# Two ties and eight row products moved in VectorE's order, in a two-layer decoder trunk

## The chip, the cores and the metric

The kernel runs on one core of one Trainium2 chip. The metric is the device time of one execution in microseconds (us). Before the change it is 683.57 us, the median of 3 runs (683.51 to 684.01).

The core has five engines that run side by side, each through its own list of instructions in a fixed order: TensorE (PE in the profile; PEld is its loading of weights), VectorE (DVE), ScalarE (ACT), GpSimd (POOL) and SyncE (SP), which here only issues loads. They wait for each other on semaphores.

## The reference, cut to what matters

Two layers work on 256 tokens of width 1024, all in float32. Each layer has a mixer and an MLP. Both begin with an RMSNorm whose result is scaled and shifted by numbers worked out from a conditioning vector c:

```python
mod = c_act @ w_ada[l] + b_ada[l]
sh_m, sc_m, gt_m, sh_f, sc_f, gt_f = jnp.split(mod[:, None, :], N_MOD, axis=-1)
h = rms_norm(x, g_pre_mix[l]) * (1.0 + sc_m) + sh_m
y = token_mixer(h, w_in[l], g_moba_out[l], g_dsa_out[l], w_out[l], cos, sin)
x = x + gt_m * rms_norm(y, g_post_mix[l])
h = rms_norm(x, g_pre_ffn[l]) * (1.0 + sc_f) + sh_f
y = conv_glu_ffn(h, w_up_act[l], w_up_lin[l], w_conv[l], b_conv[l], w_down[l])
x = x + gt_f * rms_norm(y, g_post_ffn[l])
```

The mixer projects h onto 3656 columns and runs two groups of attention heads: MoBA (at 256 tokens plain causal attention) and DSA, in which an indexer gives each query a score for each key and only the 64 best keys are attended. The MLP is down(gelu(conv3(h @ w_up_act)) * (h @ w_up_lin)).

## The kernel before, in words

**Split products.** Every large product runs in three passes of a reduced float32 type: each operand is split into a high part and a low rest, and hi*hi + hi*lo + lo*hi is summed in PSUM. `split` (L124 to L143) makes the parts of 128x1024 weights: ScalarE writes the high part (L141), VectorE the low one (L142). Low and high tiles are named wh/wl (5 of each) or dh/dl. A weight tile `raw` holds 128x2048 numbers; six of them rotate, and SyncE issues the next load (L114) when one comes free.

**Modulation.** c times w_ada is a vector times a matrix. Part of it is done on VectorE: `gemv_v` (L183 to L194) loads a tile of transposed weights and multiplies 1024 columns by the row of c, with a running sum, one *row product* (L190) for each 128 outputs. In the first layer columns 24 to 31 of `mods` are the MLP's shift (eight products), 32 to 39 the MLP's scale (eight more), 40 to 47 the MLP's gate.

**Order of the work.** The program is written out by hand. A `Background` object holds chains of generators; at every step of the main work it ticks, and a chain that has counted down issues its next piece. A planner (the Tile scheduler) then lays each engine's list: it takes, among what it holds to be ready, what was written first. So an instruction that is ready early floats forward past earlier work that waits. There are three ways to hold it: `tc.issue_after(ins)` puts what is written in its block behind `ins` on the same engine; `pin` keeps program order; and `queue` (L352 to L358) ties each instruction to the one queued before it. None of them adds a wait: they set the order of the list. The queue holds VectorE's rotations (`rope_out`, L366, L371) and the rounds of the choice (`choose`, L450 to L460: eight rounds of MAX8 at L454 and MATCH_REPLACE at L455 for each of two token tiles).

**First layer's mixer.** While TensorE projects mv, dq, dk, dv (`project`, L388 to L413), the background runs the transposes, the indexer (L424 to L448), the choice and the attention (`attend`, L462 to L552): score products into banks 4 and 5 (L474), VectorE's mask and row minimum (L484), ScalarE's exponentials (L488), VectorE's normalising (L491, L496), transposes (L503), value products (L519). The score products of the next set need both banks back from L484.

**From mixer to MLP.** `out_first` and `out_last` are the output projection; `out_last` ends with token tile 1. `boundary` (L333 to L350) follows: for each token tile the residual (L319, L327), the statistic (L255, then GpSimd's L263 and L265), the norm on VectorE (L287), transposes (L275), modulation (L298, L301, L306 to L310). Then `project(l, "lin", ...)` takes the first four column blocks of w_up_lin as one 512-column projection: eight k of 128 rows, in four units of two k. For token tile 0 it runs hi*hi and hi*lo of k = 0 to 7 in turn, then lo*hi of all eight (`late="h"`). Matmuls into one bank stay in the order written. The four units are split ahead of `out_last` (L911), the fourth (k = 6 and 7) into wh/wl.

Of the kernel before, what the change touches and what calls it, by code (L numbers as in the profile page):

```python
# [10 lines left out]
F32 = mybir.dt.float32  # L11
# [63 lines left out]
def trunk(ctx: ExitStack, tc, plan, x, c, stream, small, rope, out):  # L75
    nc = tc.nc
# [28 lines left out]

    st = {"off": 0, "behind": ()}

# [16 lines left out]
    def split(raw, where=None, pin=False, gain=None):  # L124
# [7 lines left out]
        with ExitStack() as behind:  # L132
# [8 lines left out]
            put(nc.scalar.activation(out=hi[:, :n], in_=raw, func=AF.Copy))  # L141
            put(nc.vector.tensor_tensor(out=lo[:, :n], in0=raw, in1=hi[:, :n].bitcast(F32), op=OP.subtract))  # L142
        return hi, lo  # L143
# [38 lines left out]

    def gemv_v(l, j0, j1, gap, behind=None):  # L183

        for j in range(j0, j1, 2):
            r = load(("v_a", l, j, 2048))[0]
            for i in range(2):
                ri = r[:, 1024 * i:1024 * i + 1024]
                with tc.issue_after(behind) if behind else ExitStack():
                    nc.vector.scalar_tensor_tensor(out=ri, in0=ri, scalar=1.0, in1=crow, op0=OP.mult, op1=OP.mult,  # L190
                                                   accum_out=mods[l][:, j + i:j + i + 1])
                yield gap
        nc.vector.tensor_tensor(out=mods[l][:, j0:j1], in0=mods[l][:, j0:j1],
                                in1=scol(l, "b_ada")[:, j0:j1], op=OP.add)  # L194
# [89 lines left out]
    def norm_T(t, r, banks):  # L284
        xn = [t2(), t2()]
        for h in range(2):
            nc.vector.tensor_scalar(out=xn[h], in0=xt[:, t, 512 * h:512 * h + 512], scalar1=r, scalar2=None,  # L287
                                    op0=OP.mult)
        return [turn4(xn[h], banks[h]) for h in range(2)]
# [497 lines left out]
    for l in range(DEPTH):  # L787
# [55 lines left out]
        if l == 0:  # L843
            bg.add("sf", gemv_v(l, 24, 32, 6))
            bg.add("gt", gemv_p(l, 16, 24, 34, 16))
# [60 lines left out]
        while st["out"] < 2:  # L906
# [3 lines left out]
        out_load(4, 8)  # L910
        first = [[split(raw, "lin" if g < 1 or u < 1 else None) for u, raw in enumerate(load(*us))]  # L911
                 for g, us in enumerate(project_units(l, "lin"))]
        raws = []
# [73 lines left out]
        for i in range(NF):  # L987
            if i == 3 + 4 * l:
                bg.add("ada", gemv_v(l, 40, 48, 4))
                bg.add("ada", gate_rows(l, "ffn"))  # L990
                if l + 1 < DEPTH:
                    bg.add("ada", gemv_v(l + 1, 0, 32, 5))
# [95 lines left out]
```

## Time and profile before

| what | value |
| --- | --- |
| median of 3 runs | 683.57 us |
| profiled execution, its own time | 685.16 us |
| its span | 683.4 us |
| TensorE busy | 664.3 us, 97% |
| VectorE busy | 551.2 us, 81% |
| ScalarE busy | 423.9 us, 62% |
| mean granted clock of TensorE | 0.995 |

The profile is one execution. Its time is its span and 1.76 us around it. A time such as 78.25 is counted from the span's start. A row of a timeline gives the start, the duration, the engine, line, operation, output<-inputs, the shapes, how many such instructions were merged, and in brackets how long the engine had been idle before and who released it. An instruction's duration overlaps the next one's by some 0.08 us on VectorE, and by more on TensorE, whose ends are modelled.

### The profile page before, as it was taken

What the parts mean: (1) busy time and instruction counts of PE and PEld (TensorE: products, weight loads), DVE (VectorE), ACT (ScalarE), POOL (GpSimd) and SP (SyncE); (2) the same over time, 40 slices, a digit from 0 to 9 for tenths busy, and PEclk for the clock granted to TensorE, in tenths of its full rate; (3) what the DMA queues carried; (4) which work ended last, traced back from release to release, by engine and by line L of the source; (5) the groups of instructions that cost most, each with busy time, mean ns of one, the idle gap of its engine ahead of it and who ended that gap; (6) DMA issues with size and microseconds to landing.
All of it is one profiled execution on the core that took longest, in us unless ns stands there. A gap on an engine that the chain in (4) does not pass through costs nothing.

```text
span 683.4 us, 11282 instructions
## 1 busy us (share of the span) xinstructions
PE 664.3 (97%) x4309; PEld 570.0 (83%) x4309; DVE 551.2 (81%) x1090; ACT 423.9 (62%) x788; POOL 27.7 (4%) x56
## 2 busy tenths in 40 slices
PE   8999899998999999999999999999999999999996
PEld 5877677776999999999988776877799999999994
DVE  6899999977999999897689995677689976666553
ACT  6566686977855555555586548778595555555441
POOL 1000000102000000000020000001200000000001
PEclk9999999999999999999999999999999999999999
DMA  9999649953599999896537642446146885555001
GB/s 358 421 413 395 220 192 368 340 188 124 211 361 351 396 371 346 327 335 244 186 124 267 256 165 83 147 161 240 70 185 245 313 304 195 208 185 186 0 1 62
DMA packets 24806, 163.04 MB, mean 239 GB/s; under 512 B 3344, under 2 KB 3760, under 8 KB 6576
## 3 DMA queue, kind: packets, MB, share of 16 engines
q1 hardware_dynamic: 23472, 159.77, 62.0%
q0 software_dynamic: 704, 2.11, 1.1%
q8 instruction: 34, 0.56, 0.3%
q10 hardware_dynamic: 576, 0.43, 0.2%
q14 instruction: 20, 0.16, 0.1%
HBM read 161.24 MB, written 1.06 MB: 238 GB/s over the span
## 4 chain that ended last, share of the span: by engine, by line
PE 78%; DVE 10%; ACT 5%; issue 3%; DMA 2%; POOL 1%; POOLq 0%; DVEq 0%; ACTq 0%
PE b L578 18%; PE b L577 18%; PE b L576 18%; PE b L400 14%; DVE wl L142 3%; PE b L420 3%; DMA raw<-in_stream_dram 2%; DVE iscore L443 2%; PE b L503 2%; DVE raw L709 1%; ACT t L255 1%; PE b L377 1%; PE b L275 1%; ACT wh L137 1%; ACT t L488 1%
## 5 line engine op out<-in xcount | busy, mean ns | idle before, releaser
L142 DVE TENSOR_TENSOR wl<-raw,wh 128x1024 fp32r<-128x1024 f32 (+1 forms) x146 | 173.0, 1195 | 31.6 <-ACT wh L141 28.6
L141 ACT ACTIVATE wh<-raw 128x1024 fp32r<-128x1024 f32 (+1 forms) x146 | 149.2, 1045 | 52.3 <-PE b L578 37.6
L576 PE MATMUL b<-hh,wh 128*128 128x256 f32 x640 | 180.0, 281 | 0.0
L578 PE MATMUL b<-hl,wh 128*128 128x256 f32 x640 | 179.7, 281 | 0.0
L577 PE MATMUL b<-hh,wl 128*128 128x256 f32 x640 | 179.6, 281 | 0.0
L577 PEld LDWEIGHTS b<-hh,wl 128*128 128x128 f32 x640 | 122.5, 191 | 1.3
L576 PEld LDWEIGHTS b<-hh,wh 128*128 128x128 f32 x640 | 120.2, 188 | 1.4
L578 PEld LDWEIGHTS b<-hl,wh 128*128 128x128 f32 x640 | 120.1, 188 | 0.0
L190 DVE SCALAR_TENSOR_TENSOR raw<-raw,crow 128x1024 f32<-128x1024 f32 x72 | 86.6, 1216 | 0.8 <-DMA raw<-in_stream_dram 0.7
L400 PE MATMUL b<-wh,hh 128*128 128x512 f32 (+1 forms) x184 | 73.7, 402 | 0.2
L400 PE MATMUL b<-wh,hl 128*128 128x512 f32 (+1 forms) x184 | 69.2, 391 | 0.0
L142 DVE TENSOR_TENSOR dl<-raw,dh 128x1024 fp32r<-128x1024 f32 (+2 forms) x47 | 56.8, 1210 | 12.6 <-ACT dh L141 12.6
L141 ACT ACTIVATE dh<-raw 128x1024 fp32r<-128x1024 f32 (+2 forms) x47 | 49.5, 1058 | 26.6 <-PE b L577 26.6
L968 ACT ACTIVATE t<-b,smt 128x256 f32<-128x256 f32 x44 | 25.1, 571 | 57.3 <-PE b L578 57.3
L576 PE MATMUL b<-dh,t 128*128 128x512 f32 x152 | 59.7, 393 | 0.0
L577 PE MATMUL b<-dh,t 128*128 128x512 f32 x152 | 59.6, 392 | 0.0
L578 PE MATMUL b<-dl,t 128*128 128x512 f32 x152 | 59.1, 389 | 0.0
L400 PE MATMUL b<-wl,hh 128*128 128x512 f32 (+1 forms) x184 | 55.0, 392 | 0.0
L400 PEld LDWEIGHTS b<-wh,hh 128*128 128x128 f32 x184 | 34.8, 189 | 8.5 <-issue 1.5
L400 PEld LDWEIGHTS b<-wl,hh 128*128 128x128 f32 x184 | 34.3, 191 | 6.0 <-issue 0.2
L400 PEld LDWEIGHTS b<-wh,hl 128*128 128x128 f32 x184 | 34.0, 189 | 6.0 <-issue 0.5
L969 DVE SCALAR_TENSOR_TENSOR t<-b,smt,t 128x255 f32<-128x255 f32 x44 | 21.1, 480 | 21.0 <-ACT t L968 20.8
(172 smaller groups left out, 1101.5 us busy)
## 6 DMA issues: line engine op xcount, KB each, us to landing
raw<-in_stream_dram SPq DMA_DIRECT2D x142, 1024.0 KB, 6.5
raw<-in_stream_dram SPq DMA_DIRECT2D x7, 804.0 KB, 11.4
gate<-gated POOLq DMA_DIRECT2D x4, 512.0 KB, 8.7
raw<-in_stream_dram SPq DMA_DIRECT2D x3, 512.0 KB, 6.3
xt<-in_x_dram SPq DMA_DIRECT2D x2, 512.0 KB, 4.1
raw<-in_stream_dram SPq DMA_DIRECT2D x1, 984.0 KB, 5.0
out_dram<-xt SPq DMA_DIRECT2D x2, 256.0 KB, 2.1
raw<-in_stream_dram SPq DMA_DIRECT2D x1, 328.0 KB, 5.5
```

The costliest lines, as they stand in the source:

```text
L141: put(nc.scalar.activation(out=hi[:, :n], in_=raw, func=AF.Copy))
L142: put(nc.vector.tensor_tensor(out=lo[:, :n], in0=raw, in1=hi[:, :n].bitcast(F32), op=OP.subtract))
L190: nc.vector.scalar_tensor_tensor(out=ri, in0=ri, scalar=1.0, in1=crow, op0=OP.mult, op1=OP.mult, accum_out=mods[l][:, j + i:j + i + 1])
L400: mm = lambda l_, k, i, start=False, stop=False: nc.tensor.matmul(a[:, :n], lhsT=l_[:, k, tt], rhs=w[k][i], start=start, stop=stop)
L420: ins = nc.tensor.matmul(out, lhsT=lhsT, rhs=rhs, **flags)
L443: nc.vector.scalar_tensor_tensor(out=sc, in0=r[:, j * nk:j * nk + nk], scalar=wi[:, h:h + 1], in1=fill[:, 256 - nk:] if first else sc, op0 ...
L503: nc.tensor.transpose(tp[:, 128 * j:128 * j + 128], e[:, 128 * j:128 * j + 128], ident)
L576: nc.tensor.matmul(y, lhsT=hh, rhs=wh, start=first, stop=False)
L577: nc.tensor.matmul(y, lhsT=hl, rhs=wh, start=False, stop=False)
L578: nc.tensor.matmul(y, lhsT=hh, rhs=wl, start=False, stop=last)
L968: nc.scalar.activation(out=z, in_=p[:, :256], func=AF.Identity, scale=w2[:, i:i + 1], bias=bc[:, i:i + 1])
L969: nc.vector.scalar_tensor_tensor(out=z[:, 1:], in0=p[:, :255], scalar=w1[:, i:i + 1], in1=z[:, 1:], op0=OP.mult, op1=OP.add)
```

## The change

Three edits. (a) The fourth unit of the lin weights is, in the first layer, no longer split ahead of `out_last`; its split is written in `norm_T` of token tile 1, and VectorE's half of it is tied behind that tile's second norm instruction. (b) The row products of the MLP's gate (columns 40 to 47, both layers) are tied behind the low half of the split written last. (c) The row products of the first layer's MLP shift (columns 24 to 31) become members of `queue`, at the place where they are written.

```diff
-    st = {"off": 0, "behind": ()}
+    st = {"off": 0, "behind": (), "then": []}
...
-            put(nc.vector.tensor_tensor(out=lo[:, :n], in0=raw, in1=hi[:, :n].bitcast(F32), op=OP.subtract))
+            d = put(nc.vector.tensor_tensor(out=lo[:, :n], in0=raw, in1=hi[:, :n].bitcast(F32), op=OP.subtract))
+            st["lo"] = d.ins
...
-    def gemv_v(l, j0, j1, gap, behind=None):
+    def gemv_v(l, j0, j1, gap, behind=None, put=lambda ins: ins):
...
-                with tc.issue_after(behind) if behind else ExitStack():
-                    nc.vector.scalar_tensor_tensor(out=ri, in0=ri, scalar=1.0, in1=crow, op0=OP.mult, op1=OP.mult,
-                                                   accum_out=mods[l][:, j + i:j + i + 1])
+                after = st["lo"] if behind == "lo" else behind
+                with tc.issue_after(after) if after else ExitStack():
+                    put(nc.vector.scalar_tensor_tensor(out=ri, in0=ri, scalar=1.0, in1=crow, op0=OP.mult,
+                                                       op1=OP.mult, accum_out=mods[l][:, j + i:j + i + 1]))
...
-            nc.vector.tensor_scalar(out=xn[h], in0=xt[:, t, 512 * h:512 * h + 512], scalar1=r, scalar2=None,
-                                    op0=OP.mult)
+            d = nc.vector.tensor_scalar(out=xn[h], in0=xt[:, t, 512 * h:512 * h + 512], scalar1=r, scalar2=None,
+                                        op0=OP.mult)
+        if t and st["then"]:
+            with tc.issue_after(d.ins):
+                st["then"].pop()()
...
-            bg.add("sf", gemv_v(l, 24, 32, 6))
+            bg.add("sf", gemv_v(l, 24, 32, 6, put=queue))
...
-        first = [[split(raw, "lin" if g < 1 or u < 1 else None) for u, raw in enumerate(load(*us))]
-                 for g, us in enumerate(project_units(l, "lin"))]
+        first = [load(*us) for us in project_units(l, "lin")]
+        first[0] = [split(raw, "lin") for raw in first[0]]
+        first[1][0] = split(first[1][0], "lin")
+        if l:
+            first[1][1] = split(first[1][1])
+        else:
+
+            st["then"].append(lambda: first[1].append(split(first[1].pop())))
...
-                bg.add("ada", gemv_v(l, 40, 48, 4))
+                bg.add("ada", gemv_v(l, 40, 48, 4, "lo"))
```

## Rows read from the trace of the kernel before

**Rows 1.** The page, part 1: busy time of each engine

```profile
PE 664.3 (97%) x4309; PEld 570.0 (83%) x4309; DVE 551.2 (81%) x1090; ACT 423.9 (62%) x788; POOL 27.7 (4%) x56
```

**Rows 2.** Stretches: length, PE, PEld, DVE, ACT, POOL busy (count), clock, DMA, GB/s

```profile
74.00:82.00 8.00, 6.97 (x44) 4.96 (x42) 8.00 (x38) 4.77 (x18) 0.00 (x0) 1.00 0.30 121
83.00:86.00 3.00, 3.00 (x12) 2.60 (x11) 3.00 (x11) 1.56 (x3) 0.00 (x0) 0.50 0.80 314
...
84.00:114.00 30.00, 30.00 (x232) 22.02 (x231) 28.38 (x92) 25.89 (x54) 2.30 (x2) 0.96 0.66 260
...
158.00:166.00 8.00, 6.42 (x31) 4.66 (x31) 6.45 (x14) 5.21 (x15) 1.92 (x4) 1.00 0.65 248
...
174.00:200.00 26.00, 26.00 (x189) 24.53 (x188) 25.95 (x42) 19.18 (x30) 0.00 (x0) 1.00 0.83 309
```

**Rows 3.** Chain that ended last, from 60 to 90 us: start, us, what

```profile
78.33 1.15 DVE raw L190 x2
...
80.53 1.15 DVE raw L190 x2
```

**Rows 4.** Timeline of VectorE in the first layer's mixer, 74 to 116 us

```profile
74.54 0.28 DVE L454 MAX8 tiny<-iscore 128x8 f32<-128x128 f32 x1
...
78.25 1.22 DVE L190 SCALAR_TENSOR_TENSOR raw<-raw,crow 128x1024 f32<-128x1024 f32 x1
...
80.24 0.28 DVE L484 CUSTOM_DVE_ANT_0 t<-b,lateneg 128x128 f32<-128x128 f32 x1
...
114.27 1.21 DVE L142 TENSOR_TENSOR wl<-raw,wh 128x1024 fp32r<-128x1024 f32 x1
```

**Rows 5.** Timeline of TensorE in both mixers

```profile
80.59 1.14 PE L420 MATMUL b<-kT,qT 64*128 64x256 f32 x8 [1.03 <-DVE tiny L484]
...
82.75 1.06 PE L503 MATMUL b<-ident,t 128*128 128x128 f32 x4 [0.61 <-DVE rs L491]
...
116.73 0.39 PE L400 MATMUL b<-wl,hh 128*128 128x512 f32 x1
...
410.87 1.14 PE L420 MATMUL b<-kT,qT 64*128 64x256 f32 x8 [0.47 <-DVE tiny L484]
```

**Rows 6.** Loads: SyncE's timeline at 60 us; issues with median us to landing

```profile
60.88 2.62 SPq L114 DMA_DIRECT2D raw<-in_stream_dram  x2
...
raw<-in_stream_dram SPq DMA_DIRECT2D x142, 1024.0 KB, 6.5
```

**Rows 7.** Timeline of VectorE from the first layer's mixer to its MLP

```profile
154.09 1.22 DVE L190 SCALAR_TENSOR_TENSOR raw<-raw,crow 128x1024 f32<-128x1024 f32 x1
...
155.24 1.22 DVE L190 SCALAR_TENSOR_TENSOR raw<-raw,crow 128x1024 f32<-128x1024 f32 x1
...
156.99 1.21 DVE L142 TENSOR_TENSOR wl<-raw,wh 128x1024 fp32r<-128x1024 f32 x1
158.12 0.87 DVE L287 TENSOR_SCALAR t<-xt,tiny 128x512 f32<-128x512 f32 x2
...
165.06 0.88 DVE L287 TENSOR_SCALAR t<-xt,tiny 128x512 f32<-128x512 f32 x2 [0.97 <-POOL tiny L265]
```

**Rows 8.** Timeline of TensorE from the first layer's mixer to its MLP

```profile
158.65 1.09 PE L275 MATMUL b<-ident,t 128*128 128x128 f32 x8 [0.81 <-DVE t L287]
...
162.47 0.51 PE L400 MATMUL b<-dh,hh 128*128 128x512 f32 x1 [0.50 <-ACT hh L306]
...
163.73 0.40 PE L400 MATMUL b<-wl,hh 128*128 128x512 f32 x1
...
165.61 1.11 PE L275 MATMUL b<-ident,t 128*128 128x128 f32 x8 [0.32 <-DVE t L287]
...
167.72 0.39 PE L400 MATMUL b<-dh,hh 128*128 128x512 f32 x1
```

**Rows 9.** The first MLP's fifth weight block: its split on VectorE, its first use on TensorE

```profile
180.68 1.22 DVE L142 TENSOR_TENSOR wl<-raw,wh 128x1024 fp32r<-128x1024 f32 x1
...
191.04 0.28 PE L577 MATMUL b<-hh,wl 128*128 128x256 f32 x1
```

## The prediction, made blind

> **What bounds the kernel now.** I began with the page's busy times: TensorE is busy 97% of the span, VectorE 81%, ScalarE 62% [rows 1]. So a VectorE edit pays only where TensorE visibly pauses or runs slowly, and I looked for such places in the stretches and in TensorE's timeline, then asked the chain of waits and VectorE's timeline who caused them.
>
> The first place is the first layer's mixer. TensorE pauses 1.03 us ahead of the second set's score products, released by the mask and minimum at L484, and 0.61 us ahead of the transposes at L503, released by VectorE's normalising [rows 5]. VectorE has no idle time there: it is busy 8.00 of 8.00 us from 74 to 82 [rows 2]. The chain runs through it, and a row product (1.15 us each) lies on the chain twice, at 78.33 and 80.53 [rows 3]: the seventh product cuts into the eight L484 instructions, the eighth follows the last of them, which starts at 80.24 [rows 4]. Right after the pauses TensorE's granted clock is 0.50, that is 1.2 GHz instead of 2.4, for all of 83 to 86 us [rows 2]. So this place costs more than its pauses.
>
> The second place is the step from the first mixer to its MLP. TensorE pauses 0.81, 0.50 and 0.32 us [rows 8]. On VectorE two row products (154.09 and 155.24) and one split (156.99) stand ahead of token tile 0's norm, which starts at 158.12 [rows 7]. Elsewhere TensorE is busy nearly all the time: 26.00 of 26.00 us from 174 to 200 [rows 2].
>
> **Edit (c), the eight shift products in the queue.** In the order written, products one to six stand ahead of the choice, product seven ahead of its first round (the MAX8 at 74.54 [rows 4]), product eight between its second and third. In the trace seven runs at 78.25 [rows 4], behind two rounds and half of a third: its tile was not yet there in the planner's reckoning. The chip had it in time: the load is the second of the two that begin at 60.88 and span 2.62 us, so it is issued by 63.2, and a load lands in 6.5 us [rows 6], about 69.7. The new tie can't pull the product ahead of its tile in the planner's list; it holds the rounds back behind it. I expect the five round instructions (some 0.28 us each, about 1.1 us issued) to leave the stretch ahead of L484. All of L484 then stands ahead of product seven, and banks 4 and 5 come free 1.1 + 1.15 = 2.25 us earlier. That is more than the pause of 1.03, and the normalising moves with it, so the 0.61 goes too: 1.64 us. If TensorE doesn't pause, I expect its clock not to fall: 3 us at half clock are 1.5 us of work. Together 3.1 us.
>
> What is late next is VectorE itself, since no work is removed. The fourth split of dv starts at 114.27 and takes 1.21 [rows 4], and TensorE uses it at 116.73 [rows 5]: 1.25 us to spare. Between 84 and 114 VectorE idles 30.00 - 28.38 = 1.62 us [rows 2], which an earlier TensorE can squeeze out. So between 1.25 and 2.87 us get through. I take 2.0, near the middle, as the idle spots are waits on other engines, which move with TensorE only in part. The low end for the edit is 0 (the same list); a loss is not excluded, as the rounds move into a dense stretch, but they have until the DSA group's masks, long after dv, so I put it at no more than 0.3. The first products come behind the last rotation, a swap within VectorE's list; TensorE is covered there, so 0. Loads are not reordered.
>
> **Edit (b), the gate products.** The two products at 154.09 and 155.24 leave for the MLP, and six more keep about their place. They cost 2 x 1.22 us of VectorE under a TensorE that is busy throughout. Their tile is given back later, so a later load waits. The cover is the distance from a split to its use: the fifth block's split ends at 181.90 and is used at 191.04 [rows 9], 9.1 us. If that cover were gone, the price would be up to the 2.4 us of the products; I take 0. In the second layer the tie holds products that run deep in the MLP already: 0 as well.
>
> **Edit (a), the fourth lin split.** Ahead of tile 0's norm this frees VectorE, with (b), for 2 x 1.15 + 1.13 us. But TensorE is still in the output projection until 158.65 - 0.81 = 157.84 [rows 8], so only that 0.81 is gained, and the norm of tile 1 (165.06 [rows 7]) moves to 164.25 with its whole chain.
>
> Then comes the price. The split holds k = 6 and 7, and TensorE uses its low half at 163.73 [rows 8], **before** tile 1's norm, behind which it is now tied. Matmuls into one bank keep their order, so nothing but tile 1's transposes can fill the gap. The two norm instructions issue in some 0.80 us, so the split starts at 165.05 and ends at 166.26. TensorE arrives at 163.73 - 0.81 = 162.92, waits, does the transposes (1.11 us) from 164.80, and waits on to 166.26: pauses of 1.9 and 0.35 us. Eleven products remain of tile 0, each 0.23 us by start to start (between 163.73 and 167.72 stand these eleven, the transposes and a pause of 0.32). Tile 1 begins at 166.26 + 2.53 = 168.8 instead of 167.72: **+1.1**, the gain of 0.81 already in it. TensorE has no pause behind it to give this back. The tile's load slot is held 8 us longer, under the same cover [rows 9].
>
> **The sum** is -2.0 + 1.1 = -0.9 us. On the profiled execution's span that is 683.4 to 682.5, on its own time 685.16 to 684.3. The median of the runs is 1.59 us under that time, so 683.57 becomes **682.7**. A measurement of this kernel tells about 0.2%, 1.37 us, from no change; so the forecast is no change that can be measured, on the faster side.
>
> **What the clock may do.** After two pauses, together 1.64 us, the row of 83 to 86 us shows 0.50 [rows 2]. From 158 to 166, with 0.81 + 0.50 + 0.32, it stays 1.00 [rows 2], and a pause of 0.47 at 410.87 [rows 5] belongs to no fall that I found. The new pauses of 1.9 and 0.35 are longer than those ahead of the fall, though the ones there had half-height score products between them. So a fall is open; priced by the fall that is seen, it costs up to 1.5 us more. The Trainium skill ("TensorE: Matmul & The Clock Gate", Part 1) says that the clock follows how busy the engine has lately been, and this speaks against edit (a): by it the new wait lowers the clock too, and the sum would be -2.0 + 1.1 + 1.5 = +0.6, which is 684.2. The trace agrees with the rule at 83 us.
>
> **The rivals.**
>
> *The choice pays in full.* VectorE's idle time is squeezed out and 2.87 us get through: -2.87 + 1.1, 681.8. If the split's wait is also shorter than worked out, 681. For it speaks that both pauses are released by VectorE and that the half clock goes with them; against it VectorE's 28.38 of 30 us.
>
> *The wait for the split costs double* (the slower side). One mechanism, in the lin projection at k = 6: TensorE waits, and its clock falls to 1.2 GHz while it waits, so that tile 0's rest and the transposes run at half speed. Price 1.1 + 1.5 = 2.6 us. It decides from the point where the mixer gives back less than 1.23 us; with nothing from the mixer it is 686.2, at the middle 685.2. The same price holds if the list puts tile 1's transposes behind the waiting product. For it: the order of the two numbers 163.73 and 165.06. Against it: the clock stayed up from 158 to 166.
>
> *The queue does nothing.* The list lays the products between the same L484 instructions, as the tile is late in its reckoning either way. Then only +1.1 is left: 684.7. Against it: the rounds must now come behind product seven, which takes five instructions out from ahead of L484.
>
> **How the numbers follow.** Forecast 0.38, its own range 681.8 to 683.9; choice in full 0.20; double wait 0.20; queue idle 0.17; 0.05 for another order of the second layer's list, either side. Faster by over 0.2% (under 682.2): nearly all of the second case (0.18), the lower fifth of the forecast (0.08), a little of the rest: 0.27. Slower (over 684.9): three fifths of the third case (0.12), a third of the fourth (0.06), of the rest 0.02: 0.20. Within: 0.53. The range leaves out the ends of the second and third cases: 681.0 to 685.6.
>
> **What would show it.** In the profile after: no rows of MAX8 between 74 and the first L484, the score products and L503 in the first mixer without the pauses of 1.03 and 0.61, and 1.00 as clock in that stretch. From mixer to MLP: no L190 or L142 ahead of tile 0's norm, transposes without 0.81; then a pause of some 2 us ahead of tile 1's transposes and a hi*lo product released by VectorE's L142. If that product doesn't wait, or the first mixer keeps its pauses, I am wrong at that step. A new pause in dv's projection, released by L142, would mean VectorE gave nothing on.

## The result, and the profile of the changed kernel

The changed kernel takes **687.8 us** (median of 6 executions, 686.38 to 688.49) against 683.5 us before it on the same chip: ratio 1.0058, interval 1.0045 to 1.007. It is slower by 0.6%, and outside the range of the prediction (681.0 to 685.6). Its executions differ among themselves: two took 686.4 us, four 687.6 to 688.5, and a run below shows what one of the longer kind holds. The profiled execution took 686.39 us, its span is 684.6, so the rows that follow are those of the shorter kind.

The page's first part: nothing but the order of the work is different, the busy times are those of [rows 1].

```profile
PE 663.1 (97%) x4309; PEld 568.7 (83%) x4309; DVE 551.6 (81%) x1090; ACT 424.1 (62%) x788; POOL 27.2 (4%) x56
```

The stretches of [rows 2], columns as there:

```profile
74.00:82.00 8.00, 6.78 (x44) 5.15 (x43) 7.68 (x33) 4.96 (x18) 0.00 (x0) 1.00 0.33 129
83.00:86.00 3.00, 2.48 (x15) 1.79 (x15) 3.00 (x11) 2.81 (x4) 0.00 (x0) 1.00 0.79 251
...
158.00:166.00 8.00, 5.64 (x25) 3.98 (x26) 7.00 (x15) 5.69 (x17) 1.47 (x4) 1.00 0.00 0
...
174.00:200.00 26.00, 24.81 (x180) 23.29 (x180) 25.50 (x42) 16.84 (x27) 0.00 (x0) 1.00 0.81 300
```

The half clock of 83 to 86 us is gone (1.00 instead of 0.50), yet the kernel is slower. From 158 to 166 TensorE is busy 5.64 us instead of 6.42, and from 174 to 200, where before it had no idle time at all, 1.19 us are missing.

The diff shifts the lines: L484 is now L489, L142 stays, L190 is L192, L275 L277, L287 L289, L400 L405, L420 L425, L454 L459, L455 L460, L491 L496, L496 L501, L503 L508, L577 L582; the two convolution taps in `up`, which read a PSUM bank, are L980 and L982.

TensorE's timeline, its pauses in brackets; the first two answer to [rows 5], the next two to [rows 8], the last has no counterpart:

```profile
80.96 1.13 PE L425 MATMUL b<-kT,qT 64*128 64x256 f32 x8 [1.22 <-DVE tiny L489]
83.66 0.63 PE L508 MATMUL b<-ident,t 128*128 128x128 f32 x4 [0.52 <-DVE t L501]
...
160.67 0.50 PE L405 MATMUL b<-dh,hh 128*128 128x512 f32 x1 [0.52 <-ACT hh L311]
163.80 1.12 PE L277 MATMUL b<-ident,t 128*128 128x128 f32 x8 [1.71 <-DVE t L289]
...
180.94 0.36 PE L581 MATMUL b<-hh,wh 128*128 128x256 f32 x1 [1.19 <-ACT wh L141]
```

The pauses that the queue was to remove are still there. Ahead of tile 0's transposes there is no pause any more, and the new one ahead of tile 1's is 1.71 us. A third place that I had not looked at, in the MLP, has a pause of 1.19 us. Behind tile 1's transposes there is no second one:

```profile
165.01 0.50 PE L405 MATMUL b<-dh,hh 128*128 128x512 f32 x1
...
165.81 0.40 PE L405 MATMUL b<-wl,hh 128*128 128x512 f32 x1
```

The first of these rows begins tile 1's products, the second is the product that uses the low half of the late split; three products of tile 1 stand between the transposes and it.

VectorE's timeline says who made the pauses. In the mixer (to be held against [rows 4]):

```profile
77.65 0.29 DVE L489 CUSTOM_DVE_ANT_0 t<-b,lateneg 128x128 f32<-128x128 f32 x1
77.86 1.22 DVE L192 SCALAR_TENSOR_TENSOR raw<-raw,crow 128x1024 f32<-128x1024 f32 x1
...
79.01 0.29 DVE L459 MAX8 tiny<-iscore 128x8 f32<-128x128 f32 x1
79.21 0.27 DVE L489 CUSTOM_DVE_ANT_0 t<-b,lateneg 128x128 f32<-128x128 f32 x1
...
79.48 0.28 DVE L460 MATCH_REPLACE8 iscore<-tiny,iscore 128x128 f32<-128x128 f32 x1
...
80.64 0.26 DVE L489 CUSTOM_DVE_ANT_0 t<-b,lateneg 128x128 f32<-128x128 f32 x1
...
81.42 1.22 DVE L192 SCALAR_TENSOR_TENSOR raw<-raw,crow 128x1024 f32<-128x1024 f32 x1
```

The rounds of the choice did leave the time ahead of L489, as I had said: there is no MAX8 from 74 us to the first L489. But product seven still runs in the middle of the eight, behind the fourth (before: behind the third). The rounds that were held behind it come at once, and interleave with the last four L489. The last starts at 80.64, later than before (80.24).

Nor did the rounds, once gone, give back the 1.1 us that I had counted for them. Ahead of the first mask-and-minimum stand nine sums of the indexer. Before the change, then after it:

```profile
73.22 1.40 DVE L443 SCALAR_TENSOR_TENSOR iscore<-t,wi,iscore 128x128 f32<-128x128 f32 x4
...
77.23 0.46 DVE L443 SCALAR_TENSOR_TENSOR iscore<-t,wi,iscore 128x256 f32<-128x256 f32 x1
77.62 0.28 DVE L484 CUSTOM_DVE_ANT_0 t<-b,lateneg 128x128 f32<-128x128 f32 x1
```

```profile
72.96 4.14 DVE L448 SCALAR_TENSOR_TENSOR iscore<-t,wi,iscore 128x128 f32<-128x128 f32 x9
77.02 0.28 DVE L489 CUSTOM_DVE_ANT_0 t<-b,lateneg 128x128 f32<-128x128 f32 x1
```

With the five round instructions among them the nine sums took 4.47 us (73.22 to 77.69), without them 4.14: 0.33 us were won. The 0.32 us that VectorE is idle from 74 to 82 lie among the nine; what the sums wait for there, no row says.

Between mixer and MLP, and in the MLP (to be held against [rows 7, 9]):

```profile
155.24 0.87 DVE L289 TENSOR_SCALAR t<-xt,tiny 128x512 f32<-128x512 f32 x2
...
163.26 0.88 DVE L289 TENSOR_SCALAR t<-xt,tiny 128x512 f32<-128x512 f32 x2 [0.97 <-POOL tiny L267]
164.06 1.22 DVE L142 TENSOR_TENSOR wl<-raw,wh 128x1024 fp32r<-128x1024 f32 x1
...
176.50 1.22 DVE L142 TENSOR_TENSOR wl<-raw,wh 128x1024 fp32r<-128x1024 f32 x1
177.64 1.22 DVE L192 SCALAR_TENSOR_TENSOR raw<-raw,crow 128x1024 f32<-128x1024 f32 x1
...
178.78 0.48 DVE L980 SCALAR_TENSOR_TENSOR t<-b,smt,t 128x255 f32<-128x255 f32 x1
179.18 1.22 DVE L142 TENSOR_TENSOR wl<-raw,wh 128x1024 fp32r<-128x1024 f32 x1
180.31 0.48 DVE L982 SCALAR_TENSOR_TENSOR t<-b,smt,t 128x254 f32<-128x254 f32 x1
```

The split runs behind tile 1's norm, as written. In the MLP a split, a row product and another split run ahead of and between the two taps of the first block. The taps read PSUM bank 5 (`p = bank(4 + (i + 1) % 2)`, so blocks 0 and 2, the first and the third, share it), and the third block's first product starts at 180.94, just behind the end of the second tap at 180.79. The row names ScalarE's wh as the releaser. ScalarE's timeline has the third block's wh, the third of its kind in the MLP, 7 us earlier:

```profile
172.58 1.12 ACT L141 ACTIVATE wh<-raw 128x1024 fp32r<-128x1024 f32 x1
```

As that wh had long been done, the wait was another. A run below tests that it is the bank.

### The profile page after: what moved, and what is told of

Same layout as the page of the kernel before. It is cut to its first block, busy times and chain, and to the rows that moved or that the text cites. A ratio compares the mean times of both kernels' runs of the same rounds, so it can differ in the third digit from the quotient of the medians.

```text
span 684.6 us, 11283 instructions
## 1 busy us (share of the span) xinstructions
PE 663.1 (97%) x4309; PEld 568.7 (83%) x4309; DVE 551.6 (81%) x1090; ACT 424.1 (62%) x788; POOL 27.2 (4%) x56
## 4 chain that ended last, share of the span: by engine, by line
PE 74%; DVE 12%; ACT 7%; issue 3%; DMA 2%; POOL 1%; POOLq 0%; DVEq 0%; ACTq 0%
PE b L583 19%; PE b L581 19%; PE b L582 19%; PE b L405 12%; DVE wl L142 3%; PE b L425 2%; DVE iscore L448 2%; DMA raw<-in_stream_dram 2%; ACT t L493 1%; DVE raw L714 1%; PE b L508 1%; ACT wh L141 1%; ACT t L257 1%; DVE raw L192 1%; ACT wh L137 1%
## 5 line engine op out<-in xcount | busy, mean ns | idle before, releaser
L142 DVE TENSOR_TENSOR wl<-raw,wh 128x1024 fp32r<-128x1024 f32 (+1 forms) x146 | 173.1, 1196 | 35.9 <-ACT wh L141 33.0
L582 PE MATMUL b<-hh,wl 128*128 128x256 f32 x640 | 179.6, 281 | 0.0
L582 PEld LDWEIGHTS b<-hh,wl 128*128 128x128 f32 x640 | 122.5, 191 | 1.4
L192 DVE SCALAR_TENSOR_TENSOR raw<-raw,crow 128x1024 f32<-128x1024 f32 x72 | 86.8, 1217 | 0.0
L405 PE MATMUL b<-wh,hh 128*128 128x512 f32 (+1 forms) x184 | 73.1, 400 | 0.2
L405 PE MATMUL b<-wh,hl 128*128 128x512 f32 (+1 forms) x184 | 68.9, 390 | 0.0
L142 DVE TENSOR_TENSOR dl<-raw,dh 128x1024 fp32r<-128x1024 f32 (+2 forms) x47 | 56.8, 1211 | 11.9 <-ACT dh L141 11.8
L582 PE MATMUL b<-dh,t 128*128 128x512 f32 x152 | 59.6, 392 | 0.0
L405 PE MATMUL b<-wl,hh 128*128 128x512 f32 (+1 forms) x184 | 54.6, 390 | 0.0
L405 PEld LDWEIGHTS b<-wh,hh 128*128 128x128 f32 x184 | 34.6, 188 | 8.6 <-issue 1.5
L405 PEld LDWEIGHTS b<-wl,hh 128*128 128x128 f32 x184 | 34.0, 189 | 6.2 <-issue 0.6
L405 PEld LDWEIGHTS b<-wh,hl 128*128 128x128 f32 x184 | 33.9, 189 | 5.6 <-issue 0.2
L980 DVE SCALAR_TENSOR_TENSOR t<-b,smt,t 128x255 f32<-128x255 f32 x44 | 21.1, 480 | 17.8 <-ACT t L979 17.8
```

Of the source, the lines that this page charges most:

```text
L142: d = put(nc.vector.tensor_tensor(out=lo[:, :n], in0=raw, in1=hi[:, :n].bitcast(F32), op=OP.subtract))
L192: put(nc.vector.scalar_tensor_tensor(out=ri, in0=ri, scalar=1.0, in1=crow, op0=OP.mult, op1=OP.mult, accum_out=mods[l][:, j + i:j + i + 1]))
L405: mm = lambda l_, k, i, start=False, stop=False: nc.tensor.matmul(a[:, :n], lhsT=l_[:, k, tt], rhs=w[k][i], start=start, stop=stop)
L582: nc.tensor.matmul(y, lhsT=hl, rhs=wh, start=False, stop=False)
L980: nc.vector.scalar_tensor_tensor(out=z[:, 1:], in0=p[:, :255], scalar=w1[:, i:i + 1], in1=z[:, 1:], op0=OP.mult, op1=OP.add)
```

## The experiments

Each part of the change alone comes first, then variants. All medians are of 5 to 11 executions, but for e8, the changed kernel once more (2). For each run, **mixer** is the start of the last product of the first output projection in TensorE's timeline, and **boundary** is the time from there to the start of the MLP's first product. The changed kernel's are 156.53 and 17.05:

```profile
156.53 0.40 PE L583 MATMUL b<-wl,hh 128*128 128x512 f32 x1
...
173.58 0.28 PE L581 MATMUL b<-hh,wh 128*128 128x256 f32 x1
```

| run | what it holds | us | before, same chip | mixer | boundary |
| --- | --- | --- | --- | --- | --- |
| e1_ties | (a) and (b) | 685.67 | 683.43 | 155.84 | 17.06 |
| e2_queue | (c) | 684.14 | 683.43 | 156.57 | 16.30 |
| e3_split | (a) | 685.68 | 683.43 | 155.85 | 17.09 |
| e4_gate | (b) | **682.52** | 683.43 | 155.81 | 15.38 |
| e5_split0 | (b), (c), split behind tile 0's norm | 683.47 | 683.62 | 156.63 | 15.32 |
| e6_gate_split0 | (b), split behind tile 0's norm | 682.85 | 683.62 | 157.21 | 15.35 |
| e7_split_taps | (a), MLP splits behind the taps | 684.30 | 683.62 | 155.91 | 17.07 |
| e8_again | (a), (b), (c) | 687.22 | 683.62 | 156.61 | 18.25 |
| e9_hold | (b), products 7 and 8 late | 683.15 | 683.44 | 156.48 | 15.36 |
| e10_hold484 | the same, less late | 683.00 | 683.44 | 156.30 | 15.36 |
| e11_queue6 | (c) for products 1 to 6 only | 683.46 | 683.44 | 155.81 | 16.30 |
| e12_hold_late | e9, e5's split, 4 products written late | 683.58 | 683.57 | 156.70 | 15.35 |
| e13_late | e6, 4 products written late | 682.73 | 683.57 | 155.86 | 15.32 |
| e14_hold_tied | e12, the 4 tied | 685.05 | 683.41 | 156.60 | 16.93 |
| e16_later_scores | e6, scores written later | 683.37 | 683.41 | 156.50 | 15.34 |
| e15_y4_tied | e16, the 4 products tied | 685.01 | 683.41 | 156.57 | 16.93 |

e6's profiled execution took 684.23 us, 1.38 over its median: like [rows 2] it has a half clock in the mixer, so its 157.21 stands for that execution alone. The profile of e11, which took 683.43 us, shows the lists of the kernel before in both places without a half clock: 155.81 and 16.30.

**Which part costs.** The first four runs take the edits apart:

```diff
-            bg.add("sf", gemv_v(l, 24, 32, 6, put=queue))
+            bg.add("sf", gemv_v(l, 24, 32, 6))
...
-            first[1][1] = split(first[1][1])
-        else:
-            st["then"].append(lambda: first[1].append(split(first[1].pop())))
+        first[1][1] = split(first[1][1])
...
-                bg.add("ada", gemv_v(l, 40, 48, 4, "lo"))
+                bg.add("ada", gemv_v(l, 40, 48, 4))
```

The first hunk alone is e1, the second and third are e2, the first and third e3, the first and second e4.

> Both ties without the queue. Theory (three places, each its own price): the first mixer is as before, with its pauses and its fall of the clock; TensorE waits some 1.7 us ahead of tile 1's transposes and for the split, +1.0 us from mixer to MLP; the first row product of the gate comes ahead of the convolution's taps and TensorE pauses about 1.2 us ahead of the third block of the MLP; together +2.2, about 685.7. Rival (the queue is what costs): without it the time is that of before, 683.5.

> The queue alone. Theory: TensorE's two pauses in the first mixer stay at about 1.2 and 0.5 us, so it is a matter of the clock: 1.4 us faster where the clock stays up (682.1), up to 0.4 slower where it falls (683.9), and the runs spread between these. Rival (the queue costs): 3 us slower or more, about 687. From mixer to MLP the trace should be that of before.

> The split's tie alone. Theory: the wait for the split is paid, about +1.0 us; no row product stands ahead of the taps of the MLP's first block, but two splits do, so that the pause there is under 1.2 us or gone: 684.5 to 685.3. Rival (the clock falls in the new wait): the granted clock is 0.50 for some us behind 162, and the time is 686 or more.

> The gate products' tie alone. Theory: the products only get ahead of the taps because the wait for the split lets VectorE run ahead of TensorE; without that wait they come behind the taps, the pause of 0.81 us goes and nothing is paid: 682.3 to 683.0. Rival (the tie itself costs in the MLP): TensorE pauses about 1.2 us ahead of the third block, 683.9 to 684.7.

Against 683.43: e1 +2.24 (ratio 1.0039, 1.0026 to 1.0051), e2 +0.71 (1.0011, 1.0002 to 1.002), e3 +2.25 (1.0041, 1.0027 to 1.0055), e4 -0.91 (0.9987, 0.9978 to 0.9996). Edit (a) carries most of the loss, (c) the rest; (b) alone is a gain, and adds nothing to (a), since either of them clears the place ahead of tile 0's norm (neither e3 nor e4 has the 0.81). With the queue, 683.43 + 2.24 + 0.71 is 686.38, the time of the changed kernel's shorter executions (686.38 and 686.39). So the price of the two ties and that of the queue add up to these; the median of 687.8 lies 1.4 us higher, among the longer ones.

e4 came out as expected. e2 did not: it is above both values that I gave, its eleven executions lie within 0.45 us, and with the clock at 1.00 in the mixer, where I had 682.1, it takes 684.14. e1 has the expected time, but by luck: its mixer shows 1.00 too, not the fall that I had put there, and the cause that I gave for the MLP's pause was wrong. e3, above its range, refuted that. I had put the MLP's pause down to the gate's row product, so it should have been missing here. It is there, and so is the wait for the split:

```profile
163.12 1.11 PE L277 MATMUL b<-ident,t 128*128 128x128 f32 x8 [1.71 <-DVE t L289]
...
180.33 0.36 PE L581 MATMUL b<-hh,wh 128*128 128x256 f32 x1 [1.22 <-ACT wh L141]
```

VectorE's list of e3 has three splits there (two from 175.86, one at 178.56) and no product. What it shares with the changed kernel is that splits of later blocks stand ahead of, and between, the first block's taps; in e4 both taps stand ahead of them.

**The place of the split, and the MLP's pause.** e5 is the changed kernel with `if t and st["then"]` made `if st["then"]`, so the split follows tile 0's norm; e6 is the same without the queue. e7 is edit (a) alone with the splits of blocks 3 and 4 (counted from 0) tied behind the taps:

```diff
             if i > 2:
-                st["behind"] = ()
+                st["behind"] = () if l or i > 4 else st["tap"]
...
+            if i == 0:
+                st["tap"] = d.ins,
```

Here `d` is the second tap.

> The changed kernel with one thing different: the fourth lin split is tied behind token tile 0's norm instead of tile 1's (queue and gate products as changed). Theory (it is the place behind tile 1's norm that costs, twice: TensorE waits for the low half, and the MLP's pause follows from the order that this wait brings into VectorE's list): the split is done well before TensorE's first use of its low half, no wait of 1.7 us ahead of tile 1's transposes, no pause of 1.2 us near 179 us, no pause of 0.8 us ahead of tile 0's transposes; the queue's 0.65 us stays. Time 682.52 (gate alone) + 0.65 = 683.2, within 682.8 to 683.6. Rival 1 (any move of the split behind a norm costs, since VectorE's work between the two norms is on TensorE's path): a pause ahead of tile 1's transposes or of the modulated parts, 684 to 684.5. Rival 2 (the MLP's pause comes from the gate products or the queue): a pause of 1.2 us near 179 remains, 684.4.

> Gate products tied (edit b) and the fourth lin split tied behind token tile 0's norm, without the queue. Theory: as the gate products alone, since the 0.8 us ahead of tile 0's transposes can be won only once: 682.5, within 682.2 to 682.8, and the run before it in this list is 0.65 us above it. If the split ahead of tile 0's norm still costs something where only the gate products are gone, this is below 682.2. If the split behind tile 0's norm delays tile 1's residual, it is above 682.8.

> Edit (a) alone, and in the first layer's MLP the splits of blocks 3 and 4 are tied behind the second convolution tap of block 0. Theory (the MLP's pause is a PSUM bank given back late, since VectorE runs two splits ahead of the taps): the pause of 1.2 us near 179 us goes, the wait of 1.7 us for the low half stays; 685.68 - 1.2 = 684.5, within 684.2 to 684.8. Rival (the pause is a wait for ScalarE's high part wh, as the profile's row names it): the tie makes the splits later, so the pause stays or grows, 685.7 or more.

e5 and e7 came out inside the theory's bounds, e6 0.05 above them. e5 takes 683.47, 0.15 under the kernel before and 2.9 under the changed kernel's shorter executions: one tile earlier, and both pauses of (a) are gone, the MLP's included. e7 takes 684.30 (+0.68) with the boundary still at 17.07: the wait for the split stays, the MLP's pause goes. Its TensorE timeline has the first row below and no pause near 179 us; VectorE's, second, has the taps side by side:

```profile
163.16 1.11 PE L277 MATMUL b<-ident,t 128*128 128x128 f32 x8 [1.70 <-DVE t L289]
```

```profile
177.65 0.48 DVE L980 SCALAR_TENSOR_TENSOR t<-b,smt,t 128x255 f32<-128x255 f32 x1 [1.67 <-ACT t L979]
178.17 0.48 DVE L982 SCALAR_TENSOR_TENSOR t<-b,smt,t 128x254 f32<-128x254 f32 x1
178.57 1.22 DVE L142 TENSOR_TENSOR wl<-raw,wh 128x1024 fp32r<-128x1024 f32 x1
```

The splits are later than in e3 and the pause is gone, so it was not a wait for the splits' tiles. What is left is the bank that the taps give back. From e3 to e7, against their own baselines, 2.25 - 0.68 = 1.57 us go, somewhat more than the 1.22 of the pause.

**The longer executions.** e8 is the changed kernel once more.

> The changed kernel once more, for its profile. Two of six executions took 686.4 us, four 687.6 to 688.5. Theory: the longer ones hold a fall of TensorE's granted clock to 0.5 for some 3.4 us, which costs 1.7 us, behind the wait of 1.7 us for the low half, near 162 to 168 us; the first mixer, whose pauses are as long as in the kernel with the queue alone (eleven executions within 0.45 us of each other), shows 1.0. Rival: the fall is in the first mixer, near 80 to 86 us, as in the profiled execution of the kernel before. A profile of 686.4 us would show neither.

Its profiled execution took 687.78 us, its other one 686.67. The stretches:

```profile
83.00:86.00 3.00, 2.49 (x15) 1.72 (x15) 3.00 (x11) 2.89 (x4) 0.00 (x0) 1.00 0.75 243
...
164.00:167.00 3.00, 3.00 (x12) 2.62 (x13) 2.46 (x6) 1.98 (x6) 0.00 (x0) 0.50 0.21 33
```

The granted clock is 0.50, 1.2 GHz, from 164 to 167 us, right behind the pause of 1.69 us, and 1.00 in the mixer. The place is the one expected. The boundary is 18.25 instead of 17.05, so this fall costs 1.2 us, less than the expected 1.7. The same pause, 1.71, goes without a fall in the profiles of the changed kernel, e1 and e3: whether it comes differs from one execution to the next. That the other longer executions hold it too fits their times, 1.2 to 2.1 us above the shorter ones, but no profile shows it, and the longest have more than this fall explains.

**The queue's products.** One half of the prediction's order, all eight L489 ahead of product seven, can be made by hand. e9 ties products seven and eight behind the first set's last normalising, e10 behind its last L489; both hold edit (b) and no queue:

```diff
+            while l == 0 and j == 30 and "hold" not in st:
+                yield 1
...
                 after = st["lo"] if behind == "lo" else behind
+                if l == 0 and j == 30:
+                    after = st["hold"]
```

`hold` is set in `attend` to that instruction. e11 puts only products one to six into the queue.

> The gate products tied (edit b), no queue for the products, the lin split as before; products seven and eight of the MLP shift are held behind the first set's last normalising instruction. This gives VectorE the order that the prediction expected of the queue: all eight mask-and-minimum instructions of the first set with no row product among them. Theory (the prediction's price was right and only its order was not what the queue makes): the pauses of 1.05 and 0.61 us near 79 and 82 us go, 1.25 to 1.65 us get through: 682.5 (gate alone) - 1.45 = 681.1, within 680.7 to 681.5. Rival 1 (VectorE carries the same work, so the wait only moves: to the next set's scores, whose mask and minimum now stand behind product eight, or to dv's fourth split near 117 us): new pauses there of the same size, 682.2 to 682.8. Rival 2 (the pauses are not the row products'): they stay, 682.5.

> As the run before it, but products seven and eight are held only behind the first set's last mask-and-minimum instruction, so they stand ahead of its normalising. Theory: the pause of 1.05 us ahead of the second set's scores goes, but the normalising waits for one or two products (1.15 us each), so the pause ahead of the transposes, 0.61 us, is 0.6 to 1.8 us: about 682.5 - 1.05 + 0.6 = 682.0, within 681.6 to 682.8. If VectorE's place there didn't matter, both pauses stay and the time is 682.5.

> Only products one to six of the MLP shift are in the queue, seven and eight are free as before; no other edit. Theory (the queue's 0.65 us comes from seven and eight, behind which the rounds of the choice are held and then fall between the first set's mask-and-minimum instructions): the time of the kernel before, within 0.2 us, 683.5; the pauses at 79 and 82 us are 1.05 and 0.61 us and no pause of 0.3 us at 123 us. Rival (products one to six delay the rotations behind them, and the heads' transposes with them): 684.1.

e11 takes 683.46 against 683.44: products one to six cost nothing, so the queue's 0.7 us is the price of seven and eight. e9 takes 683.15, 0.29 under the kernel before, where (b) alone is 0.91 under: as far as it has the order that I had priced at -2.0, that order costs 0.6. It has one half of it. The rounds of the choice still stand ahead, as its VectorE shows:

```profile
76.82 0.28 DVE L463 MAX8 tiny<-iscore 128x8 f32<-128x128 f32 x1
...
77.41 0.28 DVE L493 CUSTOM_DVE_ANT_0 t<-b,lateneg 128x128 f32<-128x128 f32 x1
```

No run has both halves at once. By my account the half of e9 would have been enough for the pause of 1.05. Rival 1 came nearest, 0.35 below the time and with the wait in other places than it named. e10 (-0.44) is 0.5 above (b) alone and missed its range as well. TensorE's timeline of e9 and, below it, of e4 (lines in e9: L429 is the score products, L409 the projection, L514 the transposes, L493 the mask and minimum):

```profile
78.26 0.40 PE L409 MATMUL b<-wh,hl 128*128 128x512 f32 x1
79.23 1.14 PE L429 MATMUL b<-kT,qT 64*128 64x256 f32 x8 [0.58 <-DVE tiny L493]
81.25 0.63 PE L514 MATMUL b<-ident,t 128*128 128x128 f32 x4 [0.89 <-DVE rs L500]
...
108.45 0.51 PE L409 MATMUL b<-wl,hh 128*128 128x512 f32 x1 [0.64 <-DVE wl L142]
```

```profile
78.93 0.39 PE L405 MATMUL b<-wh,hh 128*128 128x512 f32 x1
80.37 1.14 PE L425 MATMUL b<-kT,qT 64*128 64x256 f32 x8 [1.05 <-DVE tiny L489]
...
82.54 0.63 PE L508 MATMUL b<-ident,t 128*128 128x128 f32 x4 [0.61 <-DVE rs L496]
```

The score products start 1.14 us earlier, as VectorE gives the banks back earlier, but TensorE's list isn't the old one: three projection products fewer stand ahead of the scores (the last starts at 78.26, not 78.93), and none instead of one between scores and transposes. The two pauses together are 1.47 instead of 1.66, not nought, and a new one of 0.64 stands at 107.8 behind a split. Holding two products on VectorE changed TensorE's list as well: the planner lays all lists.

**Is VectorE full, or is it TensorE's list?** e12 and e13 write the last four products of the MLP scale behind dv's projection; e14 ties them behind the last DSA normalising; e16 leaves VectorE's work alone and delays the second set's score products by four steps of the projection in the writing; e15 joins e16 and e14's tie.

```diff
-            bg.add("sf", gemv_v(l, 32, 40, 9))
+            bg.add("sf", gemv_v(l, 32, 36, 9))
...
+        if l == 0:
+            bg.add("sf", gemv_v(l, 36, 40, 2, st["dsa"]))
```

The last line is that of e14 and e15; e12 and e13 have `gemv_v(l, 36, 40, 4)` there, right behind dv's projection. The next edit is that of e16 and e15:

```diff
             yield 2
+            if masks is None and not i and "far" not in st:
+                st["far"] = 1
+                yield 4
```

> Gate products tied (edit b), the lin split behind tile 0's norm, products seven and eight held behind the first set's normalising as in the run of that name (683.15, which was 0.6 us above the gate products alone, though TensorE was 1.5 us earlier at 95 us), and the last four products of the MLP scale (columns 36 to 39, 4.9 us of VectorE) are loaded and written behind dv's projection instead of beside it. Theory (VectorE has no time to spare between 79 and 131 us, so what TensorE wins at 79 it loses again at a split that comes late): with four products out of that stretch the pause of 0.64 us near 107 us goes, and 0.8 to 1.5 us of the early gain get through to 156 us: 682.5 - 1.2 = 681.3, within 680.9 to 682.0. Rival (TensorE's time from 100 to 156 us is set by ScalarE or by the loads, not by VectorE): TensorE is back on the old time by 131 us, 682.5 to 683.2.

> As the run before it without holding products seven and eight: the gate products tied, the lin split behind tile 0's norm, four products of the MLP scale behind dv's projection. Theory: with the pauses at 79 and 82 us in place TensorE has nothing to gain from a freer VectorE later, as it had no wait there: 682.5, within 682.2 to 682.9. If VectorE delayed TensorE between 84 and 131 us by itself, this is below 682.2.

> As e12_hold_late, but the four products of the MLP scale are now tied behind the last normalising of the DSA group (in e12 the list took them back to 117 to 124 us, so nothing had left the stretch). Theory A (VectorE has no time to spare from 97 to 131 us and that is what holds TensorE): with 4.9 us less there the pauses behind 107 us go, and TensorE is at least 0.7 us earlier at 156 us than in e9_hold and e12_hold_late: 682.4 or less. Theory B (the pauses belong to where the planner's list puts the waiting products on TensorE: it follows VectorE's earlier end in its own reckoning, so the score products move forward and wait again): the pauses of 0.58 and 0.89 us at 79 and 80 us stay as in e9_hold, the one at 107.8 (a split behind four row products that are left in place) too, and the time is 682.8 to 683.5.

> VectorE's work as in e6_gate_split0 (gate products tied, lin split behind tile 0's norm), but the first layer's second set of score products is written four steps of the projection later, so TensorE's list holds 19 products ahead of it instead of 13 (six more, 1.38 us). Theory B (the pause at 79 us is TensorE's list arriving too early at the scores, not a lack of work): the pause of 1.05 us goes, the one ahead of the transposes stays within 0.6 us; about 1 us is won: 681.8, within 681.4 to 682.3. Theory A (VectorE's order sets the time of the stretch; TensorE only shifts the wait): the time of e6_gate_split0, 682.8, with the pause moved to the transposes or to a later set.

> The run before it, and the four products of the MLP scale tied behind the DSA group's last normalising. If VectorE's lack of time behind 97 us costs anything once the scores come later, this is below the run before it by 0.3 us or more; if not, the two agree within 0.3 us.

e12 (683.58, above its range and the rival's) and e13 (as expected) say nothing of the question: written late without a tie, the four products floated back to between 116 and 124 us. e14 says something. Its VectorE is free for 3.7 us of the stretch from 84 to 131, against 1.66 in e9, and TensorE is where it was, busy 46.04 and 46.03 us of it. e14 first, then e9:

```profile
84.00:131.00 47.00, 46.04 (x336) 34.37 (x336) 43.30 (x135) 37.53 (x89) 5.36 (x4) 1.00 0.75 288
```

```profile
84.00:131.00 47.00, 46.03 (x336) 34.25 (x336) 45.34 (x138) 37.65 (x88) 5.37 (x4) 1.00 0.81 307
```

The mixer ends at 156.60 instead of 156.48, and the pauses at 78.6, 80.3 and 107.8 us are e9's, which is theory B's side. But the time that e14 frees lies behind 110 us. From 100 to 110, where the pause of 0.64 stands, VectorE is as busy as in e9; e14 first, then e9:

```profile
100.00:110.00 10.00, 9.36 (x78) 6.97 (x80) 9.79 (x33) 8.27 (x14) 2.59 (x1) 1.00 0.80 297
```

```profile
100.00:110.00 10.00, 9.36 (x77) 6.97 (x78) 9.78 (x33) 8.27 (x14) 2.60 (x1) 1.00 0.79 310
```

So e14 shows that spare time behind 110 us brings nothing; ahead of it a VectorE without spare time stays a rival, tested by no run. It can't be all: e10 has no pause at 107.8, and its mixer still ends 0.49 us behind e4's. (The 685.05 of e14 comes from the tied products, the last of which now starts at 149.14, shortly ahead of tile 0's residual: boundary 16.93.) e16 removes the pause of 1.05, as theory B has it, but the one ahead of the transposes grows from 0.61 to 0.77, as theory A has it, others are new or longer, and it missed its range by 1.1 us:

```profile
82.48 0.63 PE L508 MATMUL b<-ident,t 128*128 128x128 f32 x4 [0.77 <-DVE rs L496]
83.47 0.63 PE L508 MATMUL b<-ident,t 128*128 128x128 f32 x4 [0.36 <-DVE t L501]
91.61 1.13 PE L425 MATMUL b<-kT,qT 64*128 64x256 f32 x8 [0.30 <-DVE tiny L489]
...
125.87 0.63 PE L508 MATMUL b<-ident,t 128*128 128x128 f32 x4 [0.56 <-DVE t L501]
```

e15 has e16's mixer and e14's boundary, and so is 1.64 us above e16, which neither branch of its expectation allowed for. Neither theory gives the time of this stretch. What the runs do show: the mixer ends at 155.81 in the order of the kernel before, at 155.86 in e13, which leaves the list around the second set's scores alone, and at 156.30 to 156.70 in the seven orders that change it (e2, e9, e10, e12, e14, e15, e16). Why the wait comes back each time, somewhere else, stays open, as does what the full order of the prediction would have brought.

The fastest kernel here is e4, edit (b) alone: 682.52 us, below both kernels; e13 (-0.84) and e6 (-0.77) are its equals.

## Why the prediction was wrong

The forecast was a change of -0.9 us, -2.0 for the queue and +1.1 for the split; the median moved by +4.3. Of the 5.2 us between them 2.7 are the queue (+0.71 instead of -2.0), 1.1 the ties (+2.24 instead of +1.1), and the remaining 1.4 are what the longer executions have more; in the one profile of them the clock falls. So the steps that failed are the gain of edit (c) and the end of edit (a)'s cost.

**Edit (a): size about right, its second cost missed.** I had said +1.1 for the wait for the low half. From e11 to e3 the boundary grows from 16.30 to 17.09, +0.79. The pause ahead of tile 1's transposes was 1.71 where I had 1.9, but the second one, 0.35, isn't there: "nothing but tile 1's transposes can fill the gap" was wrong, since three products of tile 1 itself, into another bank, run ahead of the one that needs the split. The step that failed is "TensorE has no pause behind it to give this back", which I took to mean that the cost ends there. It has a second part: in VectorE's list splits for later blocks come ahead of the taps of the first, and the third block waits for its bank. That is 1.2 us of pause, and the larger half of (a)'s 2.25 us: without it e7 is left with 0.68. Why the planner lays the list so, no run shows; I take it that TensorE is later in its reckoning too.

**Edit (b): the zero was wrong in the good direction.** "The gain of 0.81 already in it" credited the pause ahead of tile 0's norm to (a). e4 shows that the gate's products alone were enough, at no price in the MLP: the time falls by 0.91, and the boundary alone by 0.92 (15.38 against e11's 16.30). My cover, 9.1 us between a split and its use [rows 9], did hold: in the changed kernel TensorE has no pause between 181 and 215 us. It was the wrong cover to look at. The taps, which hold a bank, are on VectorE's list beside the splits, and the third block waits for them.

**Edit (c): order, price and the median failed at once.** "All of L484 then stands ahead of product seven" is refuted by the rows after: four of eight. The "1.1" for the rounds, in "1.1 + 1.15 = 2.25 us earlier", was 0.33. The other term, 1.15, is about right (1.14 in e9). By itself it is more than the pause of 1.05, yet in e9 a pause of 0.58 is left there, the next one is 0.89 instead of 0.61, and the time is 0.6 us above (b) alone: the step from an earlier bank to "1.64 us" failed, since TensorE's list moved with it. So "between 1.25 and 2.87 us get through" didn't hold for the half of the order that was run. Of VectorE's idle time, which made the difference between the two bounds, e14 shows that more of it behind 110 us brings nothing. And the 1.5 us of half clock could not be won in the median at all. The profiled execution before, 685.16, was one of its rare longer ones: in the later runs 15 of 123 executions of that kernel took 684.7 us or more, the rest 683.3 to 683.9, and the profile of e11, which took 683.43, has 1.00 in that place. So I counted the fall twice: as a gain of the change, and in the 1.59 us by which the median lies under the profiled execution. Without it, even my own mechanism had 1.64 us to give at most. The queue is +0.7.

**The rivals.** "The queue does nothing" was the right one for its list: products between the same L484 instructions. It missed that the held rounds would come between them as well. "The wait for the split costs double" is seen in e8, and by the times it may be in most executions of the changed kernel; its price in e8 is 1.2 us where I had 1.5. The Trainium skill ("TensorE: Matmul & The Clock Gate", Part 1) says that the clock follows how busy the engine has lately been. The place of the fall in e8 agrees, 0.50 behind 1.69 us of pause; that the same pause passes at 1.00 in four other profiles shows that such a pause alone doesn't settle it. I had this rival at 0.20 together with a mixer that gives something back. The sum that came, 0.7 + 2.25 and some 1.4 more in four of six executions, lies above each of my cases, because I let each of them have at most one thing go wrong.

**What was seen as predicted:** no MAX8 ahead of the first L489; neither L192 nor L142 ahead of tile 0's norm, and transposes without the 0.81; a pause of about 2 us ahead of tile 1's transposes; clock 1.00 in the mixer. The last came by luck: I expected it because the pauses would go, and they stayed; e11, with the pauses of the kernel before, has 1.00 there too.

## What to carry to other kernels

Before a profile's features go into a sum, ask whether the median has them: a profiled execution that is longer than the median by 0.2% holds something that the others don't, and its price must not be counted as a gain. When an instruction is tied behind another, price not only who waits for it, but what the planner puts into the hole: look for instructions near it on the same list that give back a buffer or a bank, as these can have less cover than the data. Instructions taken out from between others free less than their own time where the others don't close up: 0.33 us here instead of 1.1. And a pause between two engines is not a sum of free microseconds: here every order that shortened one of the mixer's pauses lengthened another or made a new one.

## What was unexpected of the hardware

Executions differ in whether TensorE's clock falls behind the same pause: at 1.69 us of pause it went to 1.2 GHz in one profile (e8), and at 1.70 and 1.71 it stayed at 2.4 GHz in four, one of them of the same kernel. In the mixer, behind 1.04 and 0.60 us, it fell in e6's profile and not in e1's (0.50 and 1.00 from 83 to 86 us). The first fall costs 1.2 us (18.25 - 17.05), the second 1.4 (e6's profiled execution less its median, 684.23 - 682.85).
